# Multi-query attention on one core: queries loaded and turned for two pairs of heads at a time

## The chip, the cores and the metric

The kernel runs on one core of one Trainium2 chip. The metric is the device time of that core in microseconds, from the start to the end of one execution. Before the change it is 775.36 us, the median of 3 runs (774.22 to 776.4).

A core has five engines with a queue of instructions each: TensorE (PE, matmuls; its weight loads are listed as PEld), VectorE (DVE), ScalarE (ACT), GpSimd (POOL) and SyncE (SP, which here only starts DMAs). Engines wait for each other and for DMAs by semaphores.

## The reference

```python
# q: 8 x 1024 x 16 x 64, k and v: 8 x 1024 x 64, all float32
q = q.transpose(0, 2, 1, 3)
scores = np.matmul(q, k.transpose(0, 1, 3, 2)) / np.sqrt(64)     # k and v shared by all 16 heads
weights = np.exp(scores - np.max(scores, axis=-1, keepdims=True))
weights = weights / np.sum(weights, axis=-1, keepdims=True)
out = np.matmul(weights, v).transpose(0, 2, 1, 3)
```

There are 8 batches and 16 heads, and all heads of a batch share one set of keys and values. The shift by the maximum cancels in the division, and the kernel leaves it out.

## The kernel before

**Tiling.** Two heads make a pair, so there are 8 pairs in a batch and 64 in all; p counts them. A pair's queries are 1024 rows of 2 x 64 numbers. The 1024 keys are cut into 8 tiles of 128 and the 1024 queries into 2 halves of 512. A *unit* is one key tile against one half of the queries: `score` (line 382) makes two matmuls of it, one for each head, with the keys as weights (`k2t`) and the turned queries (`qt`) as the moving operand. Each result lies in one of three PSUM buffers `sc_0` to `sc_2`, as 128 keys x 2 heads x 512 queries.

**Exponentials.** Most units go to ScalarE (`exp_act`, line 398), which takes one unit in one instruction and writes fp16 weights `wt`. The others go to VectorE (`exp_dve`, lines 410 to 428), which computes the exponential by integer arithmetic on the bits of an fp16 number, in one instruction for each unit and four steps for each key tile.

**Weighted values.** `value` (line 441) multiplies the weights with the values, to which a column of ones is added, so that the sum of the weights falls out as well. `reciprocal` (line 454) and `normalise` (line 463) divide on VectorE, and line 476 stores a pair's output through SP.

**Queries.** The scores need queries with the head dimension on the partitions, so they must be turned. For every pair but the first, `load_q` (line 336) starts a DMA from POOL's queue that reads float32 and writes fp16 (`qn`, 1024 rows of 128 numbers). `trans_q` (line 345) then starts a DMA on SP that transposes it within SBUF (`qt`). `qn` has four buffers and `qt` three. `begin(w)` is called ahead of the first score of pair w: it loads pair w + 3 and turns pair w + 2.

**The first pair** is treated on its own, so that work begins early. `load_first` (line 349) loads it as float32 (`qf`), and the first batch's keys (`kn`), by plain DMAs. `turn_first` (line 360) casts both on VectorE (lines 364 and 367), turns them by TensorE against an identity (lines 375 and 378) and copies them from PSUM (line 376 on VectorE for the keys, line 380 on ScalarE for the queries). The opening lines are

```python
load_first()
load_q(1)
load_v(0)
load_q(2)
trans_q(1)
scale_v(0)
```

and only then does `turn_first` claim its tile `qn[0]`.

**Order.** A planner (`plan`, line 51) simulates TensorE, ScalarE and VectorE with estimated costs and writes out one order for all scores, exponentials, steps, value matmuls and divisions. That order is fixed for PE, ACT and DVE (line 503). A scheduler places the DMAs on POOL and SP, assigns buffers, and adds the waits: a tile that gets a used buffer waits until the last reader of the tile before it is done. Within an engine the instructions run in order, so one that waits holds back all behind it.

**Names in the trace.** Tiles have numbers behind their names: `qn_120` and `qt_126` are pair 0 (turned by TensorE), `qn_104` and `qt_110` are pair 1, `qn_108` and `qt_148` are pair 2.

The softmax here doesn't subtract the row's maximum and nothing guards it: scores larger than these inputs give would overflow.

## Time and profile before

| | us | instructions |
|---|---|---|
| span of the profiled execution | 773.4 | 29898 |
| PE busy | 733.9 (95%) | 13520 |
| DVE busy | 714.7 (92%) | 1001 |
| ACT busy | 756.2 (98%) | 823 |
| POOL busy | 107.7 (14%) | 113 |
| queue of POOL's DMAs (q0) | 26.2% of the 16 DMA engines | 80080 packets |
| queue of SP's DMAs (q1) | 33.0% of the 16 DMA engines | 149600 packets |
| first exponential on ACT starts | 9.18 | |

Busy time is the time in which at least one instruction of the engine runs. TensorE's clock was granted at 0.996 of full speed on average. PE's busy time is modelled, and its instructions overlap.

### The profile page before, as it was taken

Reading aid. Unit: us, or ns where it says so; the run is one execution under the profiler, and the core shown is the slowest. Engines: PE = TensorE matmul, PEld = TensorE weight load, DVE = VectorE, ACT = ScalarE, POOL = GpSimd, SP = SyncE. Lnnn points to the kernel's source line nnn. Section 1 sums busy time; section 2 is a strip of 40 time slices with the busy share of each in tenths; the row PEclk is TensorE's granted clock in tenths of the full one; section 3 lists DMA queues with packets and bytes.
Section 4 is the critical chain, followed back from the end, with each engine's and each line's share of the span. In section 5 each row is a group of like instructions: output and inputs, shape, how many; then the busy total and the mean of one; then the engine's idle time right before and its main releaser. Section 6 shows DMA issues by size and latency. Waiting matters only on the chain.

```text
span 773.4 us, 29898 instructions
## 1 busy us (share of the span) xinstructions
PE 733.9 (95%) x13520; PEld 488.8 (63%) x13520; DVE 714.7 (92%) x1001; ACT 756.2 (98%) x823; POOL 107.7 (14%) x113
## 2 busy tenths in 40 slices
PE   5999999999999999899999999999999999999997
PEld 2466666566666666566665676665676676666675
DVE  5999999999999998998999999999999989999972
ACT  6999999999999999999999999999999999999997
POOL 6500013010130101300012001030001200000000
PEclk9999999999999999999999999999999999999999
DMA  9945586356875457565695545864546475751322
GB/s 160 126 70 97 84 125 118 76 98 97 97 122 105 80 97 121 91 106 66 113 127 84 97 86 82 124 114 67 97 81 114 98 104 77 110 99 43 84 57 83
DMA packets 231136, 75.07 MB, mean 97 GB/s; under 512 B 164448, under 2 KB 231008, under 8 KB 231008
## 3 DMA queue, kind: packets, MB, share of 16 engines
q1 hardware_dynamic: 149600, 54.15, 33.0%
q0 software_dynamic: 80080, 18.36, 26.2%
q8 instruction: 105, 1.72, 0.9%
q10 hardware_dynamic: 1328, 0.66, 0.3%
q14 instruction: 23, 0.19, 0.1%
HBM read 39.58 MB, written 33.55 MB: 95 GB/s over the span
## 4 chain that ended last, share of the span: by engine, by line
ACT 55%; PE 20%; DVE 13%; issue 10%; DMA 1%; DVEq 0%; ACTq 0%
DMA kn<-in_k_dram 1%; PE acc_2_12426 L441 0%; PE acc_0_282 L441 0%; ACT wt_17848 L398 0%; PE acc_2_16352 L441 0%; PE acc_2_11044 L441 0%; PE acc_0_10862 L441 0%; PE acc_2_7901 L441 0%; PE acc_2_3681 L441 0%; PE acc_2_13021 L441 0%; PE acc_0_10280 L441 0%; PE acc_2_6786 L441 0%; PE acc_0_2610 L441 0%; PE acc_2_14405 L441 0%; PE acc_0_11953 L441 0%
## 5 line engine op out<-in xcount | busy, mean ns | idle before, releaser
L386 PEld LDWEIGHTS <-k2t_125 64*128 64x128 f16 x256 | 14.5, 97 | 22.6 <-issue 16.7
L386 PEld LDWEIGHTS <-k2t_3396 64*128 64x128 f16 x256 | 14.5, 93 | 13.6 <-issue 7.0
L386 PEld LDWEIGHTS <-k2t_1189 64*128 64x128 f16 x256 | 13.5, 93 | 12.5 <-issue 7.3
L386 PEld LDWEIGHTS <-k2t_10155 64*128 64x128 f16 x256 | 13.2, 93 | 12.4 <-issue 7.0
L386 PEld LDWEIGHTS <-k2t_14814 64*128 64x128 f16 x256 | 13.5, 93 | 11.6 <-issue 5.9
L386 PEld LDWEIGHTS <-k2t_7925 64*128 64x128 f16 x256 | 12.9, 93 | 11.6 <-issue 5.9
L386 PEld LDWEIGHTS <-k2t_5654 64*128 64x128 f16 x256 | 12.9, 93 | 11.5 <-issue 5.5
L386 PEld LDWEIGHTS <-k2t_12462 64*128 64x128 f16 x256 | 12.6, 93 | 11.8 <-issue 6.4
L375 PE MATMUL kps<-ident,k_117 128*128 128x128 f16 x8 | 1.0, 311 | 5.9 <-DVE k_117 L364 5.9
L380 ACT COPY qt_126<-qps 128x512 f16<-128x512 f16 x2 | 1.2, 585 | 4.8 <-PE qps L378 4.8
L364 DVE CAST k_117<-kn 128x512 f16<-128x512 f32 x2 | 0.8, 424 | 5.0 <-DMA kn<-in_k_dram 5.0
L375 PEld LDWEIGHTS <-k_117 128*128 128x128 f16 x8 | 0.8, 141 | 5.9 <-DVE k_117 L364 5.9
L336 POOL DMA_DIRECT2D qn_8808<-in_q_dram x1 | 0.9, 873 | 17.9 <-DMA qt_7923<-qn_7622 17.9
L336 POOL DMA_DIRECT2D qn_13351<-in_q_dram x1 | 0.9, 873 | 16.9 <-DMA qt_12460<-qn_12256 16.9
L336 POOL DMA_DIRECT2D qn_14222<-in_q_dram x1 | 0.9, 873 | 16.6 <-DMA qt_13353<-qn_13063 16.6
L380 ACT ACT_TABLE_LOAD x1 | 1.3, 1283 | 1.9 <-issue 1.9
L321 POOL TENSOR_SCALAR vals_1_91<-vn_14476 128x512 f16<-128x512 f32 x1 | 2.4, 2412 | 5.3 <-PE acc_2_13864 L441 5.3
L336 POOL DMA_DIRECT2D qn_11968<-in_q_dram x1 | 0.9, 876 | 16.2 <-DMA qt_11079<-qn_10813 16.2
L336 POOL DMA_DIRECT2D qn_16755<-in_q_dram x1 | 1.2, 1197 | 13.8 <-DMA qt_15928<-qn_15656 13.8
L336 POOL DMA_DIRECT2D qn_2625<-in_q_dram x1 | 0.9, 873 | 15.8 <-DMA qt_1739<-qn_1474 15.8
L336 POOL DMA_DIRECT2D qn_7622<-in_q_dram x1 | 0.9, 878 | 15.7 <-PE sc_1_7051 L386 15.7
L336 POOL DMA_DIRECT2D qn_11379<-in_q_dram x1 | 0.9, 873 | 15.2 <-DMA qt_10479<-qn_10151 15.2
(5805 smaller groups left out, 3490.6 us busy)
## 6 DMA issues: line engine op xcount, KB each, us to landing
qf<-in_q_dram ACTq DMA_DIRECT2D x2, 256.0 KB, 5.3
out_dram<-osb_474 SPq DMA_DIRECT2D x1, 512.0 KB, 3.8
out_dram<-osb_736 SPq DMA_DIRECT2D x1, 512.0 KB, 4.6
out_dram<-osb_1086 SPq DMA_DIRECT2D x1, 512.0 KB, 3.4
out_dram<-osb_1397 SPq DMA_DIRECT2D x1, 512.0 KB, 3.3
out_dram<-osb_1687 SPq DMA_DIRECT2D x1, 512.0 KB, 3.5
out_dram<-osb_1946 SPq DMA_DIRECT2D x1, 512.0 KB, 3.6
out_dram<-osb_2227 SPq DMA_DIRECT2D x1, 512.0 KB, 3.3
```

The source lines that it names most:

```text
L321: nc.gpsimd.tensor_scalar(out=x[:, :, 0:D], in0=st["vn"], scalar1=c, scalar2=None, op0=ALU.mult)
L336: nc.gpsimd.dma_start(out=qn[p], in_=q[b, :, 2 * hp : 2 * hp + 2, :].rearrange("(c p) h d -> p c (h d)", p=P),)
L364: nc.vector.tensor_copy(out=k16[:, :, r, :], in_=st["kn"])
L375: nc.tensor.transpose(kps[:, c, :], k16[:, c, :, :].rearrange("p r d -> p (r d)"), ident)
L380: nc.scalar.copy(out=qt[0][:, c - 3 : c + 1, :], in_=qps[:, c - 3 : c + 1, :])
L386: nc.tensor.matmul(sc[t, c][:, h, :], kst[p // HP]["k2t"][64 * h : 64 * h + 64, j, :], qt[p].rearrange("p c x -> p (c x)")[64 * h : 64 * h ...
```

## The change

The queries are loaded and turned for two pairs (four heads) at a time, from pair 2 on; pairs 0 and 1 stay single. A function `quad` says which pairs go together. A load then reads 1024 bytes in a row in place of 512, and there are half as many loads on POOL and half as many transposing DMAs on SP.

The tiles become twice as large, with room for two pairs, and all of `qn` and of `qt` share this size. To keep to the memory, `qn` goes from four buffers to two and `qt` from three to two. `begin(w)` acts on even w alone: it loads pairs w + 4 and w + 5 and turns pairs w + 2 and w + 3. The turned tile holds the two pairs interleaved, in blocks of 128 queries, so a score matmul reads its 512 queries as four runs of 128 with gaps of 128 between them, where it read one run of 512.

```diff
-    qp = ctx.enter_context(tc.tile_pool(name="qp", bufs=4))
-    qtp = ctx.enter_context(tc.tile_pool(name="qtp", bufs=3))
+    qp = ctx.enter_context(tc.tile_pool(name="qp", bufs=2))
+    qtp = ctx.enter_context(tc.tile_pool(name="qtp", bufs=2))
...
+    def quad(p):
+        return (p,) if p < 2 else (p & ~1, p | 1)
+    def queries(pool, tag, p, more):
+        t = pool.tile([P, 2 * NKT + more, P], FP16, tag=tag, name=f"{tag}{p}")
+        return t[:, 0 : NKT * len(quad(p)), :]
...
     def load_q(p):
-        if p >= NP or p in qn:
-            return
-        b, hp = divmod(p, HP)
-        qn[p] = qp.tile([P, NKT, 2 * D], FP16, tag="qn", name=f"qn{p}")
+        ps = quad(p)
+        b, hp = divmod(ps[0], HP)
+        qn[ps[0]] = queries(qp, "qn", p, 0)
         nc.gpsimd.dma_start(
-            out=qn[p],
-            in_=q[b, :, 2 * hp : 2 * hp + 2, :].rearrange("(c p) h d -> p c (h d)", p=P),
+            out=qn[ps[0]].rearrange("p (c r) x -> p c (r x)", r=len(ps)),
+            in_=q[b, :, 2 * hp : 2 * hp + 2 * len(ps), :].rearrange(
+                "(c p) h d -> p c (h d)", p=P),
         )
     def trans_q(p):
-        if p >= NP:
-            return
-        qt[p] = qtp.tile([P, NKT + 1, P], FP16, tag="qt", name=f"qt{p}")[:, 0:NKT, :]
+        ps = quad(p)
+        t = queries(qtp, "qt", p, 1)
         nc.sync.dma_start_transpose(
-            out=qt[p], in_=qn[p].rearrange("p c x -> p (c x)")
+            out=t, in_=qn[ps[0]].rearrange("p c x -> p (c x)")
         )
+        for r, x in enumerate(ps):
+            qt[x] = t.rearrange("p (c r) x -> p c r x", r=len(ps))[:, :, r, :]
...
-        qn[0] = qp.tile([P, NKT, 2 * D], FP16, tag="qn", name="qn0")
+        qn[0] = queries(qp, "qn", 0, 0)
...
-        qt[0] = qtp.tile([P, NKT + 1, P], FP16, tag="qt", name="qt0")[:, 0:NKT, :]
+        qt[0] = queries(qtp, "qt", 0, 1)
...
-                qt[p].rearrange("p c x -> p (c x)")[
-                    64 * h : 64 * h + 64, c * QC : (c + 1) * QC
-                ],
+                qt[p][64 * h : 64 * h + 64, 4 * c : 4 * c + 4, :],
...
     def begin(w):
-        load_q(w + 3)
-        trans_q(w + 2)
+        if w % 2 == 0:
+            if w + 4 < NP:
+                load_q(w + 4)
+            if w + 2 < NP:
+                trans_q(w + 2)
```

## The prediction, made before the changed kernel ran

> **What bounds the kernel now.** I read the busy table of the page first, then the stages by window, then ScalarE's waits, then the opening in order of time, and last the DMA issues.

> ```profile
> PE 733.9 (95%) x13520; PEld 488.8 (63%) x13520; DVE 714.7 (92%) x1001; ACT 756.2 (98%) x823; POOL 107.7 (14%) x113
> ```

> ACT (ScalarE, the exponentials of line 398) is busy for 756.2 of 773.4 us. Where are the 17 us in which it is not? The stages, columns: window, its length, busy us and instructions of PE, PEld, DVE, ACT, POOL, then clock, DMA share, GB/s:

> ```profile
> 0.00:9.18 9.18, 2.63 (x20) 1.90 (x21) 2.21 (x5) 2.42 (x4) 4.98 (x17) 1.00 1.07 171
> 9.18:40.00 30.82, 26.67 (x270) 12.19 (x268) 28.06 (x30) 29.18 (x33) 17.76 (x16) 1.00 1.23 131
> 40.00:690.00 650.00, 628.32 (x11711) 420.99 (x11708) 622.33 (x870) 646.13 (x704) 85.01 (x81) 1.00 0.61 97
> 690.00:760.00 70.00, 67.58 (x1330) 46.89 (x1328) 58.49 (x87) 70.00 (x78) 0.00 (x0) 1.00 0.31 70
> ```

> From 40 to 760 us ACT is busy all but 3.9 us: its 820 exponentials in a row are the kernel. A DMA there can only gain if ACT waited for it, and ACT's waits name TensorE alone, none above 1.3 us after the first exponential (the list of ACT's waits). The one long stretch without exponentials is the 9.18 us before the first one. Whatever moves that first exponential moves the end by as much, since the orders of PE, ACT and DVE are written out by hand and the three instruction streams of the changed program are the same, instruction for instruction, as those of the program before. The opening, in order of time (start, duration, engine, line):

> ```profile
> 1.41 1.02 POOL L336 DMA_DIRECT2D qn_104<-in_q_dram  x1 [0.21 <-issue]
> 2.75 0.90 POOL L336 DMA_DIRECT2D qn_108<-in_q_dram  x1
> ...
> 5.73 0.42 DVE L367 CAST qn_120<-qf 128x512 f16<-128x512 f32 x1
> ...
> 7.23 0.51 DVE L367 CAST qn_120<-qf 128x512 f16<-128x512 f32 x1 [1.08 <-DMA qf<-in_q_dram]
> 7.37 0.58 ACT L380 COPY qt_126<-qps 128x512 f16<-128x512 f16 x1 [4.17 <-PE qps L378]
> ...
> 8.35 1.31 SPq L345 DMA_TRANSPOSE qt_110<-qn_104  x1
> ...
> 8.63 0.58 ACT L380 COPY qt_126<-qps 128x512 f16<-128x512 f16 x1 [0.67 <-PE qps L378]
> 9.18 1.02 ACT L398 ACTIVATE wt_153<-sc_0_150 128x1024 f16<-128x1024 f32 x1
> ```

> [...] Here pair 0 does not wait for pair 1: each has one of four buffers of its own, and pair 1 is turned on the SP queue from 8.35 us, after pair 0's casts. How long a turn takes, from issue to landing:

> ```profile
> qt_110<-qn_104 SPq DMA_TRANSPOSE x1, 3.2
> ...
> qt_4302<-qn_4011 SPq DMA_TRANSPOSE x1, 6.0
> ...
> qt_5377<-qn_5107 SPq DMA_TRANSPOSE x1, 3.0
> ...
> qt_6815<-qn_6532 SPq DMA_TRANSPOSE x1, 5.9
> ```

> It is 3.0 us when little else moves, and up to some 6 us beside other transfers (7.4 and 7.7 us for two in the crowded opening).

> [...] line 424's step takes 0.66 us at 36.0 us, with POOL idle, and 1.10 us at 20.6 us, beside a POOL instruction. [...] the change reads the queries in runs of 128 elements, 256 bytes, so three jumps in a matmul of 512 columns. No run here shows that yet.

> **The change, part by part.**

> *Half as many loads and turns.* From pair 2 on, 62 loads and 62 turns become 31 and 31. POOL's issue of a load is 0.87 us (most rows of line 336), so POOL drops about 31 x 0.87 = 27 us. POOL is 14% busy and nobody waits for it, so that alone is worth nothing. [...] I set each step of line 421 and line 424 that ran beside a query load against the median of its line. The excess comes to 0.9 + 2.5 = 3.4 us over the whole kernel; half as many loads spare about 1.7 us of DVE. DVE is not the bound (92%, and ACT is 100% busy from 690 us on while DVE has 11.5 us free), so only part of it becomes ACT time. I take 0.6 us; the ends are 0 and the 3.9 us that ACT is idle between 40 and 760 us.

> *DMA traffic.* The DMA share is 0.61 in the long stage and no exponential waits for a DMA. Larger pieces gain nothing.

> *Later turns.* With two buffers of two pairs, pairs w+2 and w+3 are turned once the scores of w-1 are done, a whole two pairs (2 x 12.1 us, 773.4/64 each) ahead of use. A double turn is at most some 2 x 6 us. It is hidden by the exponentials of those two pairs. Pair 2's turn waits for pair 0's scores to leave their buffer; those end about 10 us after the first exponential (pair 1's first score is at 20.0 us, against 9.18) and pair 2 starts at 33.0 us in the trace, 13 us later. A double turn of 6 to 10 us fits. Stores queued on SP behind a turn were already queued so (lines 345 and 476 alternate in the trace), and three output buffers cover it.

> *The strided query operand* (line 389's slice becomes four pieces). 2048 score matmuls of 0.38 us[...], with the upper end in the rivals.

> *Two buffers instead of four for the queries as loaded.* This is the part that costs. In program order the tiles are pair 1, then pairs 2 and 3, then pair 0. With two buffers the third has none free. The changed program's list of waits says so: the first cast of qn_120 waits for its own load and also for the completions of pair 1's load and of pair 1's turn. So the first cast moves from 5.73 us to the landing of qt_110. The turn is still issued at 8.35 us (it waits for qn_104 alone, loaded first). It landed 3.2 us later before, but the load that follows qn_104 is now twice as large (1 MB read in place of 512 KB) and will still be moving. Bounds: 3.2 us (no disturbance) and 6.0 us (the dear turns above). I take 4.2 us: landing at 12.55 us.

> From the first cast to the first exponential, in the new order: both casts back to back; four transposes of PE start after the first one, at +0.45, and take 0.63; then ACT's first copy starts at +1.1, and from that copy to the first exponential the trace shows 9.18 - 7.37 = 1.81 us. Sum 2.9 us. The copy of the turned keys (0.68 us on DVE, queued behind the casts) ends at about +1.5 and stays beside this. So the first exponential comes at 12.55 + 2.9 = 15.45 us, 6.3 us later than now (bounds 5.3 and 8.1).

> Behind the waiting cast on DVE stands the copy of the turned keys, behind that every score; PE and ACT have nothing else to do meanwhile. Nothing hides it.

> **Sum.** 775.4 + 6.3 - 0.6 = 781.1 us.

> **The rivals.**

> *A, late start paid back.* The start costs 5.3 us but a lighter POOL removes most of ACT's stalls, 3.9 us of idle: 775.4 + 5.3 - 3.9 = 776.8, no difference that shows. For it: the stalls end with TensorE, which often waits for DVE. Against it: only some of them lie near a query load, and others come from the fixed order.

> *B, faster.* The wait is overlapped or turns out short, pair 0 starts within 1 us of now, and the lighter POOL gives 3.9 us: 775.4 + 1 - 3.9 = 772.5. Against it: a turn issued at 8.35 us cannot land before 5.73 us, and the wait is in the program.

> *C, much slower.* The strided operand or the double turn costs TensorE. If a score matmul lengthened by 5%, 1024 pairs of them by 0.02 us give 20 us on an engine that is 95% busy; half of it on the path gives 781.1 + 10 = 791. For it: PE has little slack. [...]

> **How the numbers follow.** The forecast, slower by 4 to 9 us: 0.80. C: 0.05. A: 0.10. B: 0.05. Slower by over 0.3% (over 777.7 us) is forecast and C, 0.85; within it is A, 0.10; faster is B, 0.05. The range runs from A's 776.8, taken as 777.0, to the upper bound of the start with no gain, 775.4 + 8.1 = 783.5, with 1 us for stalls that fall otherwise: 784.5.

> **What would show it.** In the changed profile the first cast of qn_120 is released by the turn qt_110, at about 12.5 us, and the first exponential stands near 15.4 us. Time from the first exponential to the end, 764.2 us before (773.4 - 9.18), should be within about 2 us of that. POOL should be busy for some 80 us. The prediction is wrong if the first exponential stays near 9 us, if score matmuls are longer than 0.39 us in the long stage, or if ACT shows waits at the first scores of even pairs.

## The result, and the profile after

The changed kernel takes 778.94 us (median of 4 runs, 778.83 to 780.77), the kernel before 774.80 us in the same comparison (4 runs, 774.22 to 776.40). The ratio is 1.0056, 95% interval 1.0033 to 1.0078: slower by 4.1 us at the medians, and by 2.6 to 6.0 us by the interval. Slower was forecast, by 4 to 9 us, so the result lies at the low end of the forecast. The interval reaches down to the prediction's bound of 0.3% and not below it.

The busy table of the changed kernel:

```profile
PE 733.0 (94%) x13520; PEld 488.1 (63%) x13520; DVE 712.0 (92%) x1001; ACT 755.5 (97%) x823; POOL 78.0 (10%) x82
```

The instruction counts of PE, DVE and ACT are those of before. POOL lost 31 instructions and 29.7 us. ACT does the same 755.5 us of work, so the longer span is time in which ACT does nothing. Where, the stages say (columns: window, its length, busy us and instructions of PE, PEld, DVE, ACT, POOL, then clock, DMA share, GB/s):

```profile
0.00:9.18 9.18, 1.04 (x8) 0.77 (x8) 0.76 (x2) 1.28 (x1) 5.09 (x17) 1.00 1.06 179
9.18:40.00 30.82, 23.17 (x186) 9.39 (x187) 23.33 (x26) 24.76 (x28) 12.22 (x12) 1.00 1.05 123
40.00:690.00 650.00, 628.70 (x11734) 421.81 (x11730) 622.10 (x872) 647.17 (x706) 60.66 (x54) 1.00 0.55 98
690.00:760.00 70.00, 67.57 (x1308) 46.30 (x1307) 60.91 (x89) 70.00 (x78) 0.00 (x0) 1.00 0.27 63
```

The windows are the same clock times as for the kernel before. In the first two, ACT is busy 1.28 + 24.76 = 26.04 us, where it had 2.42 + 29.18 = 31.60 us: 5.56 us of it are gone before 40 us have passed. From 40 us on, nothing was lost (647.17 us against 646.13 us). POOL has a third less to do there and the DMA share fell from 0.61 to 0.55, and the two together brought ACT no more than about 1 us.

The opening of the changed kernel in order of time (start, duration, engine, line; in brackets how long the engine had been idle, and what ended that):

```profile
5.07 0.76 DVE L374 CAST k_117<-kn 128x512 f16<-128x512 f32 x2 [5.07 <-DMA kn<-in_k_dram]
...
8.41 1.31 SPq L353 DMA_TRANSPOSE qt_110<-qn_104  x1
...
12.34 0.76 DVE L377 CAST qn_120<-qf 128x512 f16<-128x512 f32 x2 [6.50 <-DMA qt_110<-qn_104]
...
13.02 0.69 DVE L386 COPY k2t_125<-kps 128x1024 f16<-128x1024 f16 x1
...
15.27 1.02 ACT L406 ACTIVATE wt_153<-sc_0_150 128x1024 f16<-128x1024 f32 x1
```

The third line carries the case. VectorE casts the keys at 5.07 us, and then it sits idle for 6.50 us, until pair 1's turn has landed, although the data that it is to cast (`qf`, which landed by 7.2 us before) have been there for 5 us. It waits for the *place*, not for the data: `qn_120` has been given pair 1's buffer, and the turn is that buffer's last reader. The first exponential starts at 15.27 us instead of 9.18, 6.09 us later.

The chain that ended last, by its first two pieces, says the same from the other end (start, length, what):

```profile
1.41 6.99 DMA qn_104<-in_q_dram
8.41 3.80 DMA qt_110<-qn_104
```

Pair 1's load and turn, which the first exponential never needs, are now the start of the path that sets the time. ACT's list of waits differs from before only in that place; the longest wait of an exponential still is 1.3 us (columns: us in total, times, longest):

```profile
ACT qt_126 L390 <- PE qps L388: 10.9, 2, 10.3
ACT L390 <- issue: 1.9, 1, 1.9
ACT wt_10181 L406 <- PE sc_0_10178 L396: 1.3, 1, 1.3
```

### The profile page after: what moved, and what is told of

Same layout as the page of the kernel before. It is cut to its first block, busy times and chain, and to the rows that moved or that the text cites. A ratio compares the mean times of both kernels' runs of the same rounds, so it can differ in the third digit from the quotient of the medians.

```text
span 777.2 us, 29784 instructions
## 1 busy us (share of the span) xinstructions
PE 733.0 (94%) x13520; PEld 488.1 (63%) x13520; DVE 712.0 (92%) x1001; ACT 755.5 (97%) x823; POOL 78.0 (10%) x82
## 4 chain that ended last, share of the span: by engine, by line
ACT 59%; PE 18%; issue 10%; DVE 10%; DMA 1%; POOL 0%; DVEq 0%; POOLq 0%; ACTq 0%
DMA qn_104<-in_q_dram 1%; DMA qt_110<-qn_104 0%; PE acc_0_278 L449 0%; ACT wt_17724 L406 0%; PE acc_0_10782 L449 0%; PE acc_2_16236 L449 0%; PE acc_2_7845 L449 0%; PE acc_2_3653 L449 0%; PE acc_2_6738 L449 0%; PE acc_0_2590 L449 0%; PE acc_2_14301 L449 0%; PE acc_2_10114 L449 0%; DVE z_9442 L418 0%; DVE z_16499 L418 0%; DVE z_9805 L418 0%
## 5 line engine op out<-in xcount | busy, mean ns | idle before, releaser
L396 PEld LDWEIGHTS <-k2t_3368 64*128 64x128 f16 x256 | 14.5, 93 | 13.6 <-issue 7.7
L396 PEld LDWEIGHTS <-k2t_14706 64*128 64x128 f16 x256 | 13.4, 93 | 11.6 <-issue 6.0
L344 POOL DMA_DIRECT2D qn_10997<-in_q_dram x1 | 0.9, 873 | 29.9 <-DMA qt_10403<-qn_9811 29.9
L344 POOL DMA_DIRECT2D qn_13255<-in_q_dram x1 | 1.4, 1359 | 25.0 <-DMA qt_12647<-qn_12168 25.0
L344 POOL DMA_DIRECT2D qn_3695<-in_q_dram x1 | 0.9, 873 | 28.7 <-DMA qt_3094<-qn_2605 28.7
L321 POOL TENSOR_SCALAR vals_1_91<-vn_14372 128x512 f16<-128x512 f32 x1 | 2.4, 2425 | 12.5 <-issue 12.5
L344 POOL DMA_DIRECT2D qn_2605<-in_q_dram x1 | 1.2, 1168 | 25.0 <-DMA qt_2025<-qn_1462 25.0
L321 POOL TENSOR_SCALAR vals_1_88<-vn_12172 128x512 f16<-128x512 f32 x1 | 2.3, 2344 | 11.8 <-issue 11.8
L344 POOL DMA_DIRECT2D qn_1462<-in_q_dram x1 | 0.9, 873 | 26.1 <-DMA qt_919<-qn_408 26.1
```

What stands on the lines that cost most here:

```text
L321: nc.gpsimd.tensor_scalar(out=x[:, :, 0:D], in0=st["vn"], scalar1=c, scalar2=None, op0=ALU.mult)
L344: nc.gpsimd.dma_start(out=qn[ps[0]].rearrange("p (c r) x -> p c (r x)", r=len(ps)), in_=q[b, :, 2 * hp : 2 * hp + 2 * len(ps), :].rearrang ...
L396: nc.tensor.matmul(sc[t, c][:, h, :], kst[p // HP]["k2t"][64 * h : 64 * h + 64, j, :], qt[p][64 * h : 64 * h + 64, 4 * c : 4 * c + 4, :], ...
```

## The experiments

The theory: the whole loss is the wait of pair 0's first cast for pair 1's buffer, and the rest of the change (double loads, double turns, strided operand, fewer buffers) is worth nothing that can be measured. The rivals: the rest costs or gains several us that the wait hides. Ratios are to the kernel before, on the same chip, with their 95% intervals. Experiments 1, 2, 4 and 5 share one chip, 3, 6 and 7 another, 8 and 9 a third.

**1. The change without the wait.** Pair 0 gets a buffer of its own.

```diff
-        qn[0] = queries(qp, "qn", 0, 0)
+        qn[0] = qp.tile([P, NKT, 2 * D], FP16, tag="q0", bufs=1, name="qn0")
```

> The changed kernel, with pair 0's cast queries in a buffer of their own (2 KB more per partition), so that the first cast no longer waits for pair 1's turn. Theory (the start wait is the whole loss, the rest of the change is worth 1 to 1.5 us): the first exponential is back at 9.2 us and the time is 773.4 us, ratio to before 0.998. Rival (the strided operand, the double turns or the two buffers cost something in the long stage): the time stays above 776 us. Rival (the start is not on the path): 778.9 us, as the changed kernel.

Measured: 773.99 us, ratio 1.0000 (0.9991 to 1.0010). VectorE and ScalarE in the opening of this run:

```profile
5.16 0.76 DVE L374 CAST k<-kn 128x512 f16<-128x512 f32 x2 [5.16 <-DMA kn<-in_k_dram]
5.84 0.42 DVE L377 CAST qn<-qf 128x512 f16<-128x512 f32 x1
7.29 0.61 DVE L377 CAST qn<-qf 128x512 f16<-128x512 f32 x1 [1.03 <-DMA qf<-in_q_dram]
```

```profile
9.29 7.44 ACT L406 ACTIVATE wt<-sc 128x1024 f16<-128x1024 f32 x8
```

The first cast follows the keys' casts without a gap, and the only idle time left, 1.03 us, ends with the data `qf` themselves. The first exponential is back at 9.29 us, and so is the time. One buffer of 2 KB for each partition removes the loss. All the rest of the change together is worth 0, give or take 0.8 us.

**2. The wait without the change.** The kernel before, but pairs 0 and 1 share one buffer. Loads, turns and operand stay single.

```diff
-        qn[p] = qp.tile([P, NKT, 2 * D], FP16, tag="qn", name=f"qn{p}")
+        first = dict(tag="qa", bufs=1) if p == 1 else dict(tag="qn")
+        qn[p] = qp.tile([P, NKT, 2 * D], FP16, name=f"qn{p}", **first)
...
-        qn[0] = qp.tile([P, NKT, 2 * D], FP16, tag="qn", name="qn0")
+        qn[0] = qp.tile([P, NKT, 2 * D], FP16, tag="qa", bufs=1, name="qn0")
```

> The kernel before, in which only pair 0 and pair 1 share one buffer for their loaded queries; loads, turns, operands and all other buffers as before. Theory: the first cast waits for pair 1's turn, which lands at 11.6 us as before (3.2 us after its issue), the first exponential comes at 14.5 us, 5.3 us later, and the time is 774.8 + 5.3 - 0.5 = 779.6 us. Rival (the wait is absorbed later): under 777 us.

Measured: 778.93 us, ratio 1.0061 (1.0045 to 1.0076). VectorE and ScalarE in its opening:

```profile
11.51 1.21 DVE L368 CAST qn<-qf 128x512 f16<-128x512 f32 x2 [5.85 <-DMA qt<-qn]
```

```profile
14.89 1.94 ACT L399 ACTIVATE wt<-sc 128x1024 f16<-128x1024 f32 x2
```

The wait alone costs 4.8 us at the medians (3.5 to 5.9), the whole change 4.1 us (2.6 to 6.0), each against the kernel before in its own comparison: within the noise the wait is the whole loss. With pair 2's load single, the cast starts 0.8 us sooner (11.51 against 12.34 us). Of this, 0.2 us is that the turn was issued sooner (8.20 against 8.41 us). The rest bears out, for this step alone, that a neighbour twice as large slows the turn: it took 3.2 us in the kernel before and 3.7 to 3.8 us in the changed kernel and experiments 1 and 3.

**3. One more buffer for all.** `qn` with three buffers instead of two.

```diff
-    qp = ctx.enter_context(tc.tile_pool(name="qp", bufs=2))
+    qp = ctx.enter_context(tc.tile_pool(name="qp", bufs=3))
```

> The changed kernel with three buffers in place of two for the loaded queries (4 KB more per partition). Theory: as with the buffer of its own, no wait at the start, first exponential at 9.2 to 9.3 us, 774.0 us. Rival (the second buffer and not the first cast is what counts, that is, later loads also wait): a difference of over 1 us to the kernel with the buffer of its own, in the long stage.

Measured: 773.90 us, ratio 0.9996 (0.9987 to 1.0005); the first exponential starts at 9.21 us. The third tile in program order finds a free buffer, and that it is twice as large as needed does not matter. Both this run and experiment 1 are level with the kernel before on their chips, so a third buffer gives the later pairs nothing that can be measured.

**4. The strided operand alone.** The kernel before, with `qt` spread so that a score matmul reads four runs of 128 with gaps.

```diff
-        qt[p] = qtp.tile([P, NKT + 1, P], FP16, tag="qt", name=f"qt{p}")[:, 0:NKT, :]
+        qt[p] = qtp.tile([P, NKT, 2, P], FP16, tag="qt", name=f"qt{p}")[:, :, 0, :]
...
-                qt[p].rearrange("p c x -> p (c x)")[
-                    64 * h : 64 * h + 64, c * QC : (c + 1) * QC
-                ],
+                qt[p][64 * h : 64 * h + 64, 4 * c : 4 * c + 4, :],
```

> The kernel before, with the turned queries written with gaps of 128 between blocks of 128 and read so by the scores; all else as before. Theory (runs of 256 bytes cost nothing): 774.8 us, score matmuls of 0.37 to 0.39 us in the long stage. Rival (the strided operand slows TensorE by 5%): over 785 us.

Measured: 774.33 us, ratio 1.0000 (0.9991 to 1.0008). The group of score matmuls in this run, and then in the run of experiment 2, whose operand is contiguous (count, busy us, mean ns, idle time before them):

```profile
L386 PE MATMUL sc<-qt,k2t 64*128 64x512 f16 x2048 | 348.2, 387 | 28.3 <-ACT wt L396 15.9 <-DVE z L408 5.2
```

```profile
L387 PE MATMUL sc<-qt,k2t 64*128 64x512 f16 x2048 | 348.6, 387 | 25.9 <-ACT wt L399 16.4 <-DVE z L411 2.3
```

387 ns with the gaps and 387 ns without: the three jumps in a read of 512 columns cost nothing that shows here. That they would cost nothing was the author's estimate in the forecast, which no run had shown before.

**5. Single loads with all else as in experiment 1.** Two loads for each double tile, and so a contiguous operand.

```diff
-        nc.gpsimd.dma_start(
-            out=qn[ps[0]].rearrange("p (c r) x -> p c (r x)", r=len(ps)),
...
+        for r in range(len(ps)):
+            nc.gpsimd.dma_start(
+                out=qn[ps[0]][:, NKT * r : NKT * r + NKT, :],
...
-            qt[x] = t.rearrange("p (c r) x -> p c r x", r=len(ps))[:, :, r, :]
+            qt[x] = t[:, NKT * r : NKT * r + NKT, :]
```

> As the kernel with a buffer of its own for pair 0, but each double tile is filled by two loads, one for each pair, laid out so that a score reads 512 queries in one run; turns stay double. Theory (the small gain of the long stage comes from GpSimd issuing half as many loads[...]): the gain goes, 774.8 us as before. Rival (the gain comes from fewer turns and fewer semaphores): 773.4 us. Rival (the strided operand costs): faster than the kernel with the own buffer by over 1 us.

Measured: 774.29 us, ratio 1.0002 (0.9993 to 1.0012). POOL is busy for 107.3 us again, where experiment 1 has 78.6 us, and the time is the same within 0.1%. The halved loads, which were the purpose of the change, bring nothing here.

**6. No loads or turns after pairs 2 and 3.** All later scores read the queries of these two pairs again, so this run leaves out the loads and turns of 60 pairs.

```diff
-            if w + 4 < NP:
-                load_q(w + 4)
-            if w + 2 < NP:
-                trans_q(w + 2)
+            if w == 0:
+                trans_q(2)
+            elif w + 2 < NP:
+                qt[w + 2], qt[w + 3] = qt[2], qt[3]
```

> The kernel with the buffer of its own, without any query load or turn after pairs 2 and 3: all later pairs compute on the queries of pairs 2 and 3 (the output is theirs, not the later pairs'). It shows what the query loads and turns of the long stage can cost at most. Theory (next to nothing[...]): 772.5 to 773.7 us. Rival (loads and turns weigh on the long stage): 770 us or less.

Measured: 773.47 us, ratio 0.9989 (0.9980 to 0.9998). The long stage of this run, and then of experiment 1 (columns as above):

```profile
40.00:690.00 650.00, 628.74 (x11743) 421.85 (x11742) 620.79 (x871) 647.21 (x707) 33.92 (x26) 1.00 0.21 53
```

```profile
40.00:690.00 650.00, 628.75 (x11719) 421.36 (x11715) 620.72 (x870) 646.66 (x706) 60.85 (x54) 1.00 0.54 97
```

With the DMA share down from 0.54 to 0.21 and POOL's work halved, ACT does 0.55 us more in 650 us, and even this can have another cause, since TensorE's clock dropped for 3.4 us in the trace of experiment 1 (mean clock 0.996) and not in this one (0.999; see the end). By the medians, taking away nearly every query load and turn saves 0.9 us of 774 (0.2 to 1.5). That is the ceiling of anything that can be won by loading queries more cheaply; half as many loads can win only a part of it.

**7. An earlier opening, first try: a miss.** With the wait gone, the opening is bound by its DMAs (VectorE's idle times in experiment 1, of 5.16 and 1.03 us, end with `kn` and `qf`), so the first batch's values, which are needed last, were put behind the queries of pairs 1 to 3, on GpSimd's queue (added to experiment 1).

```diff
-        nc.sync.dma_start(out=st["vn"],
+        (nc.sync if b else nc.gpsimd).dma_start(out=st["vn"],
...
     load_q(1)
-    load_v(0)
     load_q(2)
+    load_v(0)
```

> The kernel with the buffer of its own, with the first batch's values loaded from GpSimd's queue behind the first query loads[...]. Theory (the start is the lever: time moves one to one with the first exponential): the second half of pair 0's queries lands up to 1 us earlier, the first exponential is at 8.3 to 8.9 us, and the time falls by as much, to 773.3 us. Rival (a later stage takes the gain back): 774.0 us with an earlier first exponential.

Measured: 778.45 us, ratio 1.0049 (1.0036 to 1.0062). The first exponential did come earlier, at 8.91 us, but ACT's waits show one of 4.0 us that no other run has:

```profile
ACT wt L406 <- PE sc L396: 9.5, 11, 4.0
```

SyncE's queue in the same run says where that comes from (start, time of the issuing instruction):

```profile
24.31 1.24 SPq L327 DMA_TRANSPOSE k2t<-k  x1
27.73 0.37 SPq L311 DMA_DIRECT2D vn<-in_v_dram  x1
28.21 8.12 SPq L353 DMA_TRANSPOSE qt<-qn  x2
```

The load of later values (line 311) waits until GpSimd has scaled the values before, which are late now; behind it on the queue stands the double turn of pairs 2 and 3. It is issued at 28.21 us, where experiment 1 has it at 22.64 us, while pair 2 begins 24 us after the first exponential, near 33 us. TensorE waited for the turn, and ACT for TensorE:

```profile
36.93 0.45 PE L396 MATMUL sc<-qt,k2t 64*128 64x512 f16 x2 [3.95 <-DMA qt<-qn]
```

Right after that wait TensorE ran at half its clock (0.51, columns as in the stages):

```profile
37.10:40.50 3.40, 3.40 (x35) 1.74 (x34) 1.56 (x2) 2.08 (x3) 1.75 (x2) 0.51 0.91 129
```

Set beside those of the kernel before, the exponentials fell back by 5.3 us from the 24th to the 27th: 4.1 us over the wait and 1.2 us behind it. The wait in SyncE's queue was paid by what stood behind it, and the clock added to it.

**8. The same with all values on GpSimd's queue,** so that SyncE's queue holds no load that waits.

```diff
-        (nc.sync if b else nc.gpsimd).dma_start(out=st["vn"],
+        nc.gpsimd.dma_start(out=st["vn"],
```

> As the run in which the first batch's values load from GpSimd's queue, but with every load of values there, so that SyncE's queue no longer holds a load that waits for GpSimd's scaling. Theory (the 4 to 5 us stall of that run came from the double turn of pairs 2 and 3 standing behind such a load): the double turn is issued near 25.5 us instead of 28.2 us and lands near 32 us, ScalarE shows no wait above 2 us after the first exponential, the first exponential stays at 8.9 us, and the time is 773.8 us (ratio 0.999 to 1.000). Rival (the turn is late for another reason, the turn of the next batch's keys ahead of it or the transfers beside it): the turn still lands after 34 us, ScalarE still waits some 3 to 4 us near 33 us, time 777 to 778.5.

Measured: 773.80 us, ratio 0.9991 (0.9981 to 1.0001). SyncE's queue and ACT's waits:

```profile
23.51 1.24 SPq L327 DMA_TRANSPOSE k2t<-k  x1
24.85 11.16 SPq L353 DMA_TRANSPOSE qt<-qn  x2
```

```profile
ACT wt L406 <- PE sc L396: 4.1, 8, 1.3
```

The turn is issued at 24.85 us and the stall of 4 us is gone, so its place in the queue was the cause. The first exponential stands at 8.87 us, as foreseen. Against the kernel before, the interval just touches 1.

**9. A shorter opening still.** In addition, the second half of pair 0's turned queries gets a PSUM bank of its own and is copied by VectorE, beside ScalarE's copy of the first half.

```diff
-        qps = psp.tile([P, NKT, P], FP16, tag="acc1", name="qps")
+        qps = [psp.tile([P, 4, P], FP16, tag=x, name=f"qps{x}") for x in ("acc1", "sc2")]
...
-            nc.tensor.transpose(qps[:, c, :], qn[0][:, c, :], ident)
-            if c % 4 == 3:
-                nc.scalar.copy(out=qt[0][:, c - 3 : c + 1, :], in_=qps[:, c - 3 : c + 1, :])
+            nc.tensor.transpose(qps[c // 4][:, c % 4, :], qn[0][:, c, :], ident)
+        nc.scalar.copy(out=qt[0][:, 0:4, :], in_=qps[0])
+        nc.vector.tensor_copy(out=qt[0][:, 4:8, :], in_=qps[1])
```

> The run before, and the second half of pair 0's turned queries in a PSUM bank of its own, copied by VectorE beside ScalarE's copy of the first half. Theory (the opening up to the first exponential is serial, so what it is shortened by comes off the end): first exponential at 8.3 to 8.5 us, time 773.2 us (ratio 0.998 to 0.9995), if the double turn is in time. Rival: the earlier start makes the double turn too late, and ScalarE waits for it by as much as was gained, or by more: time 774 us or above.

Measured: 772.95 us at the median of 20 runs, but three of them took 778.6 to 779.4 us; ratio 0.9995 (0.9980 to 1.0010), which leaves open whether it is faster. In the profiled run the keys' cast began 0.57 us later than in experiment 8 (5.32 against 4.75 us, when the keys landed), and the first exponential stood at 8.93 us: from that cast on, 3.61 us instead of 4.12, so the edit does save 0.5 us. It missed the 8.3 to 8.5 us that I expected because the landing of the keys moved by as much. The runs near 779 us cost what the late double turn cost in experiment 7; that it is the cause was not shown, since none of them was profiled. Their mean clock was 0.990, but three runs near 773 us had 0.988 to 0.991 as well. No version here that computes the right output is shown to beat the kernel before.

## Why the prediction was right, point by point

**The wait, right.** The step was: the first cast of `qn_120` moves to the landing of pair 1's turn, at 12.55 us (11.55 to 14.35). It moved to 12.34 us; the turn took 3.8 us, where 4.2 were taken. Experiments 1 and 2 show it to be the whole loss: without it nothing is left, and alone it gives 4.8 us at the medians.

**From the cast to the first exponential, right.** 15.27 - 12.34 = 2.93 us, against 2.9. Nothing hid it: VectorE (for 6.50 us), TensorE (5.89 us) and ScalarE (10.27 us) all stood still until the cast or what followed from it.

**What the rest gains, mis-sized.** The forecast was 2.2 us too high. Of that, 0.6 is the kernel before, which came out at 774.80 us instead of 775.36, and 0.2 is the start (6.09 instead of 6.3). The other 1.4 us belong to the term "I take 0.6 us", for which the medians give 774.80 + 6.09 - 778.94 = 1.95 us, within the bounds of 0 to 3.9. In the profiled executions the time from the first exponential to the end fell by 2.3 us, from 764.2 to 761.9, a little over the 2 us that were allowed. Setting each exponential of the one trace beside the same one of the other shows that they keep step for hundreds in a row, and lose it in three places:

- 0.6 us by the 20th exponential. Pair 0's exponentials now run when the opening's transfers and GpSimd's scaling are partly over: VectorE's first four steps of lines 421 and 424 (429 and 432 after the change) took 3.98 us in all before, with POOL at work beside most of them, and 3.31 us in the changed kernel. Experiment 2, the only other late start, has the loads of before and gained 0.8 us here (its four steps took 3.17 us). Of the eight other traces with an early start, none gained over 0.1 us (3.61 to 4.26 us). So this goes with the late start, which is paid back a little, and it isn't owed to the halved loads.
- 0.6 us at one key tile near 326 us. The three DVE steps there, in the kernel before and after:

```profile
320.68 1.02 DVE L421 TENSOR_SCALAR wt_7138<-z_7167 128x2048 uint16<-128x2048 uint16 x1
321.62 1.09 DVE L424 TENSOR_SCALAR u_7222<-z_7167 128x2048 uint16<-128x2048 uint16 x1
...
322.74 1.51 DVE L427 TENSOR_TENSOR m_7223<-u_7222 128x2048 f16<-128x2048 f16 x1
```

```profile
326.12 0.68 DVE L429 TENSOR_SCALAR wt_7086<-z_7115 128x2048 uint16<-128x2048 uint16 x1
326.72 1.08 DVE L432 TENSOR_SCALAR u_7170<-z_7115 128x2048 uint16<-128x2048 uint16 x1
...
327.83 1.23 DVE L435 TENSOR_TENSOR m_7171<-u_7170 128x2048 f16<-128x2048 f16 x1
```

  3.62 against 2.99 us. Before, a query load, a cast and a scaling of values ran one after the other on POOL from 320.3 to 324.0 us, beside all three steps; in the changed kernel only a load fell there (325.9 to 327.3 us), beside the first two, of which the second alone was long. So four of the five steps that ran beside a POOL instruction were long: 1.02 us against 0.68 us in the changed kernel, 1.09 and 1.08 us against 0.66 us with POOL idle (at 36.0 us in the kernel before), 1.51 us against 1.23 us. The one of 0.68 us ran beside the load too. Why they were long was not shown. And the slow piece is gone in experiments 2 and 5 as well, which have as many loads as before: here it mattered where the POOL instructions fell, not how many there are.
- 0.9 us from 536 us on, which is chance: TensorE ran at half its clock for 3.4 us in the profiled run of before, and not in that of after (below).

So the step that was off is the reason of this term. It was to come from half as many loads beside VectorE's steps, and VectorE's busy time did fall by 2.7 us, from 714.7 to 712.0. But experiment 1 keeps the halved loads, experiment 5 undoes them, and the time is the same. In the profiled executions, what the changed kernel won back came from the late start, from where POOL's instructions fall and from the clock. The sizes of this term rest on four runs of each kernel, whose interval leaves it 0 to 3.5 us.

**No cost where none was forecast, right.** The strided operand (experiment 4: 387 ns either way) and the DMA traffic (experiment 6: 0.9 us of 774 without nearly all of it) do nothing that counts. POOL is busy for 78.0 us; the sum gave some 80. The double turns are hidden in the changed kernel (no exponential waits for more than 1.3 us), but the statement that pair 2's first one "fits" held less room than it seemed: with the early start, a turn issued 5.6 us later in SyncE's queue cost over 4 us (experiment 7).

**The rivals.** A, the late start paid back, would have been slower by 1.4 us or 0.2%; the changed kernel loses at least 0.33%, and experiment 2 at least 0.45%. The medians leave room for a payback of 0.9 to 2 us, but experiment 2's interval (3.5 to 5.9 us lost) reaches its later start (5.7 us), so the times alone do not show a payback. The traces show one of 0.6 to 0.8 us by the 20th exponential, and so the prediction's step that whatever moves the first exponential moves the end by as much holds only nearly. B and C fall with experiments 1 and 4: the change has nothing to give or take apart from its wait.

## What to carry to other kernels

When buffers are made larger and fewer, count them at the start-up and not only in the steady state: tiles that prefetch for later may take the buffers in program order ahead of the one that the first result needs, and a wait in the serial opening is paid nearly in full (4.8 us for a start 5.7 us later in experiment 2). Give the one-off first tile a buffer of its own; here 2 KB for each partition undid the loss. And before making transfers cheaper, bound what they cost at all by a run without them: here it was under 1.6 us of 774.

## What had not been expected of the hardware

**A load with runs twice as long does not take half the packet time.** GpSimd's queue, before and then after (packets, MB, share of the 16 DMA engines' span):

```profile
q0 software_dynamic: 80080, 18.36, 26.2%
```

```profile
q0 software_dynamic: 47840, 18.35, 21.0%
```

The same bytes in 40% fewer packets took 20% less of the DMA engines. Packets of 256 bytes as written took 41 ns at the median, those of 512 bytes 60 ns.

```profile
532.10:535.50 3.40, 2.09 (x19) 0.76 (x18) 3.37 (x6) 3.40 (x5) 0.28 (x1) 1.00 0.86 96
535.50:538.90 3.40, 3.40 (x41) 2.04 (x41) 3.26 (x4) 3.23 (x4) 0.00 (x0) 0.50 0.03 5
```

In the second window TensorE is busy throughout, at a clock of 0.50, and has 41 matmuls, where the changed kernel has 64 from the same point of the work on (540.20 to 543.60 us). It cost 0.9 us. TensorE did not stand still ahead of the drop: it was busy for 2.09 of the 3.40 us, and its waits for ScalarE were of 0.24 to 0.53 us. The changed kernel had the same waits at this place (2.10 of 3.40 us, from 536.80 us) and no drop.

By the record of the clock in the trace the drop lasts 3.413 us, from 535.48 us, and the record changes a whole number of such stretches after it begins: 148 and 149 stretches (505.17 and 508.59 us) in the kernel before, 217 (740.69 us) in the changed kernel. Divided into these stretches, the trace of the kernel before has TensorE busy for 61.7% of the one ahead of the drop. The next lowest between the opening and the end, from 142.9 us, has 62.3%, and no drop follows it. The lowest of the changed kernel has 62.4% (from 148.3 us), without a drop. In experiment 5 the stretches ahead of its two drops (near 147 and 536 us) have about 62%. The drop of experiment 7 follows the wait of 3.95 us. This is read from traces, with ends of matmuls that are modelled; no experiment moved it, and what sets off a drop was not shown. The kernel before and experiments 1 and 3 have one drop near 147 or 535 us (mean clock 0.996 each), 5 and 9 have two (0.994); besides the one of experiment 7, the other traces have none. A difference of 1 us between two single traces is no finding.

**In the opening TensorE runs at half pace, though the clock column says 1.00.** The record of the clock begins at 30.3 us in the kernel before, and the two score matmuls of a unit change their pace there:

```profile
28.95 0.63 PE L386 MATMUL sc_1_325<-qt_110,k2t_125 64*128 64x512 f16 x2
...
30.87 0.39 PE L386 MATMUL sc_1_361<-qt_110,k2t_125 64*128 64x512 f16 x2
```

Two units in a row start 0.40 us apart just ahead of it (28.55 and 28.95 us) and 0.22 us apart behind it (30.87 and 31.09 us). In the kernel before and in the changed kernel TensorE was busy throughout the 3.413 us ahead of the record's beginning; the fullest such stretch before that had 91.8 and 89.5%. The record begins 21.1 us after the first exponential in the kernel before, 20.4 us in the changed kernel and 18.7 us in experiment 2. Most of what the traces differ by between the 20th and the 24th exponential goes with this: experiment 2, in which full pace came 0.8 us after the 20th, gained 0.7 us over the kernel before, in which it came 2.4 us after.
